# A diffusion-transformer layer on one core: a written order for the gate/up chunks, the down-projection split by stream, and the latent values moved

## The chip, the core and the metric

The kernel runs on one core of a Trainium2 chip. The metric is the device time of one execution in microseconds (us), as the median of several runs. The core has five engines that work side by side, each through its own instruction queue in order: TensorE (matrix products, "PE" in the profile, its weight loads "PEld"), VectorE ("DVE"), ScalarE ("ACT"), GpSimd ("POOL") and SyncE ("SP"), which here issues all DMA transfers. Sixteen DMA engines move data between the chip's main memory (DRAM) and the on-chip memories: SBUF, and PSUM, into which TensorE writes.

## The reference

One layer of a flow-matching backbone over 512 latent tokens and 256 context tokens of width 1024. Every sub-layer is a "sandwich": RMS norm, shift and scale, the sub-layer, RMS norm, gate, residual. Cut to what matters here:

```python
ml = adaln(c, w_mod, b_mod)         # silu(c) @ w_mod + b_mod: nine vectors of 1024, latent tokens
mc = adaln(c_ctx, w_mod, b_mod)     # the same for context tokens (vectors 0 to 4 are used)
h  = x   + 0.5 * gate * rms_norm(swiglu(modulate(rms_norm(x,   g), shift, scale)), g2)   # FFN 1
hc = ctx + 0.5 * gate * rms_norm(swiglu(modulate(rms_norm(ctx, g), shift, scale)), g2)   # same weights
k_c, v_c = split_kv(modulate(rms_norm(hc, g), ...) @ w_in[:, K and V columns])
u = modulate(rms_norm(h, g), ...) @ w_in          # q, k, v and the gated convolution's inputs
h = h + gate * rms_norm(token_mixer(u, k_c, v_c)) # 8 heads, two softmax maps each, over 768 keys
h = h + 0.5 * gate * rms_norm(swiglu(...))        # FFN 2, latent tokens only
```

The FFN's hidden width is 2816, 22 chunks of 128. All is float32. A product is made of three passes with a high and a low part of each operand: high x high, high x low, low x high.

## The kernel before

**Splitting.** `unit` (L74) loads 512 KB of weights into a tile `wraw` (four buffers). `split` (L80) makes `whi` on ScalarE (`hi`, L62) and `wlo = wraw - whi` on VectorE (`lo`, L67), or on GpSimd for every n-th unit when `pool_share` is n.

**Who sets the order.** The program is written as one sequence, and generators (`take`, `drain`) weave side work into it. A planner then puts each engine's instructions in order at build time: by priority, which falls with the place in the text, among those that its own estimate of durations holds ready. So the order of an engine's queue can differ from the text, and is fixed when the program runs. `tc.issue_after` adds edges where the author wants them.

**Gate/up of FFN 1** (L541 to L626). Latent and context tokens are one operand of 768 columns, used as halves of 384. Chunks 0 and 1 are plain (`plain_tail`, L532). From chunk 2 on, a Strassen-like scheme needs seven products of 12 matmuls (`product`, L569) instead of eight. It takes four weight operands, made from the gate raw `rg` and the up raw `ru`: `rg` itself, a difference written over half of `ru`, the pair `s12`, and `s4`. `weights1` and `weights2` (L543 to L559) form them with four GpSimd operations (L548 to L551) and split them. The products accumulate in three PSUM tiles A (`pa`), K (`pb`) and G (`pc`); copies `n1`, `n7`, `n6` (L583, L597, L599) keep states that a later product accumulates over. `tail` (L619) runs the seventh product of a chunk in the next iteration, and `spill` (L464) writes the hidden chunk as `hh` and `hl` to `hf_dram`.

**Conditioning sums** (`mod_steps`, L474). The modulation vectors 2 to 8 are matrix-vector products that VectorE makes: `macc = mraw * scalar + macc` (L490), 512 columns at a time, two columns blocks q for each vector m, for the latent (v=0) and, for m up to 4, the context stream (v=1). TensorE adds over the partitions with a matrix of ones; VectorE then multiplies by an identity matrix (L512) and reduces (L516), which turns the summed row into columns. Vectors 2 to 4 are made in the gate/up loop, 5 to 8 in the first part of the down-projection.

**Down-projection of FFN 1** (`down`, L658). Two passes over the 22 chunks. Part 1 makes all eight output blocks for the context (256 columns) and latent blocks 0, 1, 2 (512 columns); part 2 makes latent blocks 3 to 7, with 640 of 1024 weight columns, and beside it the context's chain runs.

**The chain** (`sandwich`, L1149): norm, gate and residual for eight blocks, a second norm, then modulation into high and low parts. Most of its steps are VectorE and ScalarE work with two short visits to TensorE per norm (`rstd_steps`, L107).

**Context keys and values** (L709 to L747). `kv_ctx_k` for 8 heads, then `kv_ctx_v` for 4 pairs of heads, with the latent chain beside them (`pool_share` 2).

**Attention** (L750 to L947). `gen_v` (L779) makes the latent values of a pair of heads, `gen_qk` its keys and queries, `gen_conv` the convolution branch; a running budget (`slot`, `due`) spreads this work over 32 score blocks.

## Time and profile before

| | us |
|---|---|
| median of 3 runs (1700.87 to 1707.27) | 1704.58 |
| the profiled execution | 1702.55 |
| its span in the profile | 1700.5 |
| gate/up loop, 92 to 422 | 330 |
| down-projection, part 1, 422 to 561 | 139 |
| down-projection, part 2, 561 to 641 | 80 |
| context keys and values, 641 to 710 | 69 |
| attention, 710 to 1079 | 369 |
| the rest of the layer, 1079 to 1700.5 | 621.5 |

TensorE is busy 1597.5 us (94%), VectorE 1070.5 (63%), ScalarE 711.1 (42%), GpSimd 324.4 (19%). The stages were cut at the first and last matmuls of their output tiles. A row of a timeline is: start, duration, engine, line, operation, output from inputs, count, and in brackets how long the engine stood idle before and what released it. A row of the instruction groups ends with the total busy time, the mean in ns, and the idle time before them. A row of the waits gives who waited for whom, the total in us, how often, and the longest. A row of DMA issues gives the size of one and the median us from issue to landing. Because matmuls are pipelined, a TensorE that shows as busy can still be slower than its best; the spacing of starts tells.

### The profile page before, as it was taken

The page shows a single profiled execution, that of the slowest core. Times are in us where ns is not written, and L with a number is a line of the kernel's source. Part 1 is how long each engine was busy: PE and PEld are TensorE (multiplying, and loading weights), DVE is VectorE, ACT ScalarE, POOL GpSimd, SP SyncE. Part 2 cuts the span into 40 slices and gives each one's busy share as a digit, 9 for nine tenths or more (in the row PEclk, how much of TensorE's full clock was granted, in tenths as well). Part 3 has the DMA queues.
Part 4 walks back from the last instruction along what each step waited for, and adds up shares of the span by engine and source line. Part 5 has one row for each costly group of instructions (what it writes and reads, how often), then busy time and mean ns, then how long its engine had stood idle before and what let it go on. Part 6 is the DMA issues. An engine that isn't in the chain of part 4 may idle for free. (4 is left out here: it accounts for less than half of the span.)

```text
span 1700.5 us, 23561 instructions
## 1 busy us (share of the span) xinstructions
PE 1597.5 (94%) x8962; PEld 1423.9 (84%) x8962; DVE 1070.5 (63%) x1492; ACT 711.1 (42%) x1125; POOL 324.4 (19%) x241
## 2 busy tenths in 40 slices
PE   5989999998988997999999999999999999999996
PEld 4889989898867786978888988878889998888886
DVE  5698889874566637677777776473347844333345
ACT  4543444344111434545555555452237732222234
POOL 3555555562000105310000000000002100000003
PEclk9989999999999997999999999999999999999998
DMA  9144444435898885874544453643246743232321
GB/s 366 45 154 156 149 167 151 160 120 170 313 320 320 288 279 180 259 206 118 155 130 143 118 146 103 217 150 103 95 135 200 246 151 112 84 114 91 92 79 50
DMA packets 117583, 281.98 MB, mean 166 GB/s; under 512 B 12768, under 2 KB 43616, under 8 KB 117472
## 3 DMA queue, kind: packets, MB, share of 16 engines
q1 hardware_dynamic: 117472, 280.50, 50.8%
q8 instruction: 70, 1.15, 0.3%
q14 instruction: 41, 0.34, 0.1%
HBM read 233.79 MB, written 34.08 MB: 158 GB/s over the span
## 5 line engine op out<-in xcount | busy, mean ns | idle before, releaser
L62 ACT CAST whi<-wraw 128x1024 fp32r<-128x1024 f32 (+2 forms) x266 | 266.5, 1004 | 513.7 <-PE pa L90 94.9
L67 DVE TENSOR_TENSOR wlo<-wraw,whi 128x1024 fp32r<-128x1024 f32 (+2 forms) x258 | 327.1, 1269 | 189.0 <-ACT whi L62 177.4
L90 PE MATMUL f<-xs,whi 128*128 128x512 f32 x640 | 199.9, 393 | 0.0
L90 PE MATMUL pa<-xs,whi 128*128 128x512 f32 (+1 forms) x704 | 195.8, 361 | 0.8 <-ACT ob L900 0.5
L90 PEld LDWEIGHTS pa<-xs,whi 128*128 128x128 f32 x704 | 126.1, 189 | 21.2 <-ACT ob L900 0.7
L490 DVE SCALAR_TENSOR_TENSOR macc<-mraw,sc,macc 128x512 f32<-128x512 f32 x140 | 131.1, 963 | 11.3 <-DMA mraw<-wmodr 10.0
L90 PEld LDWEIGHTS f<-xs,whi 128*128 128x128 f32 x640 | 118.1, 188 | 23.1
L90 PE MATMUL pa<-xs,wlo 128*128 128x512 f32 (+1 forms) x352 | 127.0, 361 | 1.5 <-DVE wlo L67 1.5
L90 PE MATMUL f<-xs,wlo 128*128 128x512 f32 x320 | 124.9, 390 | 0.0
L143 POOL TENSOR_TENSOR sqacc<-sqacc,sqt 128x256 f32<-128x256 f32 (+1 forms) x20 | 19.3, 967 | 500.3 <-ACT sqt L141 498.4
L90 PE MATMUL pb<-xs,whi 128*128 128x512 f32 (+1 forms) x448 | 114.4, 344 | 0.0
L676 PE MATMUL c<-hh,whi 128*128 128x256 f32 (+1 forms) x264 | 85.5, 326 | 16.6 <-ACT whi L62 12.6
L676 PE MATMUL c<-hl,whi 128*128 128x256 f32 (+1 forms) x264 | 84.6, 321 | 3.2 <-DMA hl<-hf_dram 3.2
L90 PEld LDWEIGHTS pb<-xs,whi 128*128 128x128 f32 x448 | 78.0, 189 | 10.0
L676 PE MATMUL c<-hh,wlo 128*128 128x256 f32 (+1 forms) x264 | 84.9, 323 | 0.9 <-DVE wlo L67 0.8
L868 ACT ACTIVATE e<-s,mx 128x768 f32<-128x768 f32 x64 | 57.1, 898 | 48.1 <-DVE mx L864 44.8
L90 PE MATMUL pb<-xs,wlo 128*128 128x512 f32 (+1 forms) x224 | 77.1, 344 | 0.0
L766 POOL TENSOR_TENSOR rot<-rot,cossin 128x512 f32<-128x512 f32 x16 | 23.3, 1454 | 280.7 <-DVE rot L765 280.7
L90 PEld LDWEIGHTS pa<-xs,wlo 128*128 128x128 f32 x352 | 66.4, 189 | 11.7 <-DVE wlo L67 1.7
L676 PEld LDWEIGHTS c<-hh,whi 128*128 128x128 f32 x264 | 50.5, 191 | 25.0 <-ACT whi L62 15.1
L90 PEld LDWEIGHTS f<-xs,wlo 128*128 128x128 f32 x320 | 60.1, 188 | 12.9
L574 PE MATMUL pb<-wm,whi 128*128 128x384 f32 x208 | 54.6, 344 | 5.1 <-DVE g L537 5.1
(379 smaller groups left out, 3902.4 us busy)
## 6 DMA issues: line engine op xcount, KB each, us to landing
mraw<-wmodr SPq DMA_DIRECT2D x56, 512.0 KB, 4.3
wraw<-f2gu SPq DMA_DIRECT2D x56, 512.0 KB, 3.6
wraw<-f1gu SPq DMA_DIRECT2D x44, 512.0 KB, 3.5
wraw<-f1d SPq DMA_DIRECT2D x22, 512.0 KB, 5.8
wraw<-f2d SPq DMA_DIRECT2D x24, 384.0 KB, 3.2
hf_dram<-hh SPq DMA_DIRECT2D x22, 384.0 KB, 2.3
hf_dram<-hl SPq DMA_DIRECT2D x22, 384.0 KB, 2.3
hh<-hf_dram SPq DMA_DIRECT2D x22, 384.0 KB, 5.5
```

What stands on the lines that cost most here:

```text
L62: self.nc.scalar.copy(out=out, in_=src)
L67: (eng or self.nc.vector).tensor_tensor(out=out, in0=src, in1=hi.bitcast(F32), op=ALU.subtract)
L90: self.nc.tensor.matmul(out, lhsT=lhsT, rhs=rhs, start=start, stop=stop)
L143: eng.tensor_tensor(out=a, in0=a, in1=s, op=ALU.add)
L490: nc.vector.scalar_tensor_tensor(out=acc[:, v], in0=raw[:, k], scalar=s, in1=acc[:, v], op0=ALU.mult, op1=ALU.add)
L574: self.nc.tensor.matmul(out, lhsT=w, rhs=x, start=start and p + j == 0, stop=p == 3 and j == 2, skip_group_check=True)
L676: nc.tensor.matmul(o, lhsT=w[:, c], rhs=x[hl], start=start and f + j == 0, stop=f == NF - 1 and j == 2, skip_group_check=True)
L766: nc.gpsimd.tensor_tensor(out=rt, in0=rt, in1=cs[:, 1, :], op=ALU.mult)
L868: nc.scalar.activation(e[m], ps[:, m * NKEY:(m + 1) * NKEY], AF.Exp, scale=SCALE, bias=mx[:, 2 + m:3 + m], accum_out=mx[:, 4 + m:5 + m])
```

## The change

**A written order.** `in_order` wraps the gate/up section from the plain tails on. Afterwards it links each instruction of TensorE, VectorE, ScalarE and GpSimd to the one before it on the same engine, so the planner keeps the order of the text on these four. SP's order stays with the planner.

```diff
+    @contextmanager
+    def in_order(self):
+        cur = self.nc.cur_bb
+        n = len(cur.bb.instructions)
+        yield
+        prev = {}
+        for i in cur.bb.instructions[n:]:
+            if i.engine in self.ordered:
+                p = prev.get(i.engine)
+                if p is not None:
+                    self.tc.add_manual_dep(i, p.name, ...)
+                prev[i.engine] = i
```

**Weights of a gate/up chunk** in finer steps. Two of the four GpSimd operations go to VectorE (`w_dve`), and the splits are placed one by one. Chunk 2's weights are begun during the opening products.

```diff
+        def w_pool(f):
+            tt = nc.gpsimd.tensor_tensor
+            tt(out=s12[:, 0], in0=ru[:, :512], in1=ru[:, 512:], op=ALU.add)
+            tt(out=ru[:, :512], in0=rg[:, :512], in1=ru[:, :512], op=ALU.subtract)
+        def w_dve(f):
+            tt = nc.vector.tensor_tensor
+            tt(out=s12[:, 1], in0=s12[:, 0], in1=rg[:, :512], op=ALU.subtract)
+            tt(out=s4, in0=rg[:, 512:], in1=s12[:, 1], op=ALU.subtract)
...
+            if i == 2:
+                w_load(2)
+                w_pool(2)
+                w_dve(2)
+                w_hi(2, 0)
+                w_lo(2, 0)
+                w_hi(2, 2)
+                w_lo(2, 2)
...
+        with self.in_order():
+            plain_tail(0, ps0[0])
+            w_hi(2, 1)
+            w_lo(2, 1)
+            plain_tail(1, ps0[1])
+            cur = begin(2)
...
+                nc.scalar.copy(out=n1, in_=A)
+                if tail:
+                    product(*tail[0])
+                if more:
+                    w_load(f + 1)
+                    w_pool(f + 1)
+                    w_hi(f + 1, 0)
+                    w_lo(f + 1, 0)
+                if tail:
+                    tail[1]()
+                product(K, f, 1, 0, "t3", True)
+                if more:
+                    w_dve(f + 1)
+                if tail:
+                    tail[2]()
+                nc.scalar.copy(out=n7, in_=K)
+                product(A, f, 2, 1, "t2", False)
+                take(mods, 2)
+                if more:
+                    w_hi(f + 1, 2)
+                    w_lo(f + 1, 2)
+                nc.scalar.copy(out=n6, in_=A)
+                product(G, f, 0, 1, "b21", True)
...
+                product(A, f, 2, 0, "t1", False)
...
+                product(K, f, 1, 1, "t4", False)
+                if more:
+                    w_hi(f + 1, 3)
+                    w_lo(f + 1, 3)
+                    cur = begin(f + 1)
...
+                take(mods, 3)
```

Here `tail[0]` is the seventh product of the chunk before, `tail[1]` its silu and GpSimd multiplication, `tail[2]` its spill; `w_hi` and `w_lo` are the two halves of a split.

**Conditioning sums** are cut into an accumulating half (`mod_acc`) and a summing half (`mod_sum`). Vectors 2 and 3 stay in the gate/up loop. Vectors 4 to 8 are accumulated in part 1 of the down-projection and summed in part 2. The summed row is no longer turned by VectorE: ScalarE copies it out, a DMA writes it to DRAM, and another reads it back across the partitions.

```diff
+            row = acc[0:1, :]
+            nc.scalar.copy(out=row, in_=pm[0:1, :])
+            rd = row_dram[m, v]
+            nc.sync.dma_start(out=rd[q:q + 1, :], in_=row)
+            yield
+            if q == 0:
+                return
+            mods = (ml, mcx)[v][:, m * 8:m * 8 + 8]
+            nc.sync.dma_start(out=mods, in_=rd.rearrange("q (i p) -> p (q i)", p=P))
...
+        def mod_late():
+            for m, vs in ((4, (0, 1)), (5, (0,)), (6, (0,)), (7, (0,)), (8, (0,))):
+                for q in range(2):
+                    yield from mod_acc(fp, m, q, vs, 4 if m == 4 else None)
```

**Down-projection by stream.** Part 1 makes the eight latent blocks (eight PSUM banks, full weights, latent columns of `hf_dram`), part 2 the eight context blocks, with the full weights again and the latent chain beside it.

```diff
+        for _ in down(slice(0, 3, 2), [(p, True) for p in pl]):
+            take(mods, 5)
...
+        self.pool_share = 4
+        for f, _ in enumerate(down(slice(1, 2), [(p, d % 2 == 0) for d, p in enumerate(pcs)])):
+            if f > 0:
+                take(chain, 1 if f < 12 else 2)
+            for _ in range(3):
+                next(next(sums, iter(())), None)
```

**Values.** `gen_v` and `kv_ctx_v` give way to `values(q, ts)`, which makes a pair of heads' values for the token blocks `ts` (0 and 1 are context, 2 to 5 latent) and writes them to `v_dram`. It runs between the down-projection and attention, beside the context's chain; attention only loads them (`load_v`). Weights `wv` are read 12 times instead of 16.

```diff
+        self.pool_share = 3
+        for q in range(2):
+            values(q, [2, 3, 4, 5])
+            take(chain, 10)
+        drain(chain)
+        for q in range(2, 4):
+            values(q, [0, 1, 2, 3, 4, 5])
+        for q in range(2):
+            values(q, [0, 1])
         for j in range(NH):
             kv_ctx_k(j)
-            take(chain, 2)
-        for q in range(4):
-            kv_ctx_v(q)
-            take(chain, 4)
-        drain(chain)
...
-        drain(gen_v(0))
+        load_v(0)
```

More of the change, by code (lines that the diff above doesn't have):

```diff
@@ L692, in build @@
[L692 to L706 removed]
+        pl = [self.t(psf, [P, 512], f"b{d}") for d in range(ND)]
@@ new lines, in build @@
+        for d in range(ND):
+            if d % 2:
+                nc.vector.tensor_copy(out=yc[d], in_=pcs[d])
+            else:
+                nc.scalar.copy(out=yc[d], in_=pcs[d])
+            self.sqadd(fp, sqyc, yc[d], d, NCX)
+        for g in sums:
+            next(g, None)
+        drain(chain)
+        xc = [self.t(fp, [P, 2, NCX], f"xc{d}", F32R) for d in range(ND)]
+        xchi, xclo = [t[:, 0, :] for t in xc], [t[:, 1, :] for t in xc]
+        cx = lambda k: (xchi[k], xclo[k])
@@ L930, in build @@
                 prev = (a, at, j, qb)
-                due += slot
+                due += share
                 while due > 0:
```

368 lines of the change are left out of this document (163 added, 205 removed).

## The prediction

> **What bounds the kernel now.** I read the engines' busy time by stage first (columns: stretch, its length, then busy time and instruction count of TensorE, its weight loads, VectorE, ScalarE and GpSimd; granted clock, DMA share, GB/s). The stretches are the gate/up loop of the first FFN, its down-projection's parts 1 and 2, the context's keys and values, and attention; the change leaves the 621 us behind them alone.
>
> ```profile
> 92.00:422.00 330.00, 306.28 (x1692) 301.54 (x1692) 270.16 (x301) 140.85 (x214) 177.02 (x113) 0.97 0.45 154
> 422.00:561.00 139.00, 120.81 (x727) 105.51 (x728) 85.34 (x118) 24.34 (x27) 0.00 (x0) 0.95 0.88 311
> 561.00:641.00 80.00, 79.52 (x364) 65.25 (x362) 40.57 (x81) 30.96 (x55) 9.37 (x10) 1.00 0.88 284
> 641.00:710.00 69.00, 56.66 (x414) 55.27 (x414) 53.53 (x70) 34.20 (x55) 33.82 (x18) 0.85 0.63 203
> 710.00:1079.00 369.00, 366.64 (x2088) 320.09 (x2086) 270.47 (x430) 200.07 (x349) 23.26 (x16) 1.00 0.50 144
> ```
>
> A busy TensorE says little, because matmuls overlap. So I took their pitch from the chain that ended last and from the timeline: 24 in 2.88 us with 256 columns (0.120 each), 24 in 5.44 with 512 (0.227), and one product of 12 with 384 columns from 96.41 to 98.49, 2.08 us.
>
> ```profile
> 1347.16 2.88 PE pa L90 x24
> ...
> 1436.85 5.44 PE pb L90 x24
> ```
> ```profile
> 96.41 0.51 PE L574 MATMUL pa<-xs,whx 128*128 128x384 f32 x2
> ...
> 98.49 0.51 PE L574 MATMUL pc<-xo,whx 128*128 128x384 f32 x2
> ...
> 366.98 0.51 PE L574 MATMUL pc<-xo,whi 128*128 128x384 f32 x2
> ```
> ```profile
> 398.38 0.55 DVE L606 TENSOR_TENSOR g<-n,pc 128x384 f32<-128x384 f32 x1 [1.31 <-PE pc L574]
> ...
> 412.94 0.56 DVE L606 TENSOR_TENSOR g<-n,pc 128x384 f32<-128x384 f32 x1 [1.38 <-PE pc L574]
> ```
>
> Gate/up: a chunk f is seven products, 7 x 2.08 = 14.56 us. The product into pc starts at 98.49 for f=2 and at 366.98 for f=18: 16.78 us a chunk. The last chunks, where the conditioning sums have run out, keep 14.56 exactly (398.38 to 412.94). Over 19 intervals that is (16 x 16.78 + 3 x 14.56) / 19 = 16.43. VectorE tells why:
>
> ```profile
> 369.00:412.90 43.90, 43.90 (x255) 43.90 (x254) 23.72 (x30) 20.29 (x31) 15.59 (x12) 1.00 0.39 130
> 108.00:369.00 261.00, 241.73 (x1332) 237.63 (x1333) 226.09 (x250) 109.83 (x169) 152.94 (x96) 0.97 0.45 154
> ```
>
> With sums it is busy 226.09 of 261 us, 14.5 us a chunk; without, 23.72 of 43.9, 7.9 us. It has no spare time in which to catch up, and accumulating products wait for its evacuations (18.0 us in the first row below). Ahead of the loop TensorE stands idle twice, 2.87 and 5.07 us; the second time VectorE works on the sums for 4.78 us before the multiplication that frees bank pb.
>
> ```profile
> PEld pa L574 <- DVE u L609: 18.0, 8, 4.2
> ```
> ```profile
> 84.50 0.62 PE L574 MATMUL pa<-xe,whx 128*128 128x384 f32 x2 [2.87 <-ACT g L535]
> ...
> 92.58 1.01 PE L574 MATMUL pb<-wm,whi 128*128 128x384 f32 x2 [5.07 <-DVE g L537]
> ```
> ```profile
> 84.68 4.78 DVE L490 SCALAR_TENSOR_TENSOR macc<-mraw,sc,macc 128x512 f32<-128x512 f32 x4
> ```
>
> Down, part 1, is held by transfers: DMA share 0.88, and ScalarE waits 54.0 us for f1d. Part 2 is TensorE's: 22 x 15 x 0.227 = 75 of 80 us. The context's keys and values need 384 x 0.120 = 46.1 us and take 69: the latent chain (norm, residual, modulation) uses the same vector engines, and one stop, of 2.52 us, is shown below, and the stage's clock is 0.85. Attention keeps TensorE busy 366.64 of 369 us.
>
> ```profile
> ACT whi L62 <- DMA wraw<-f1d: 54.0, 11, 10.8
> ```
> ```profile
> 649.47 1.86 PE L90 MATMUL l<-ones,sqacc 128*128 128x1 f32 x8 [2.52 <-DVE sqacc L143]
> ```
>
> **The change, part by part.** The profiled execution took 1702.55 us around its span of 1700.5; the median of the runs is 1704.58, 2.0 more. The sum goes by the former, and 2.0 is added at the end.
>
> Opening. The plain tail of chunk 0 now comes before any sum, and the weights of chunk 2 are made during the opening products. The 2.87 stays (a ScalarE wait). Of the 5.07, about 1.5 stays, because the fixed order puts the split of the weight operand that pb needs between the two tails (a ScalarE copy of 1.05 us, rows below, then VectorE's low half): -3.6 (bounds 0 and -5.1).
>
> Loop. The sums taken here fall from three modulation vectors to two, spread over all 20 chunks: 64 accumulations, 3.2 a chunk. Two subtractions move from GpSimd to VectorE.
>
> ```profile
> L549 POOL TENSOR_TENSOR wraw<-wraw,wraw 128x512 f32<-128x512 f32 x18 | 31.8, 1768 | 1.4
> L548 POOL TENSOR_TENSOR s<-wraw 128x512 f32<-128x512 f32 x18 | 31.2, 1732 | 33.7 <-issue 21.8 <-DMA wraw<-f1gu 5.0 <-DVE wlo L67 3.6
> ...
> L622 POOL TENSOR_TENSOR u<-u,g 128x384 f32<-128x384 f32 x19 | 29.1, 1534 | 38.6 <-ACT g L621 33.8 <-DVE macc L490 4.8
> ```
> ```profile
> L62 ACT CAST whi<-wraw 128x1024 fp32r<-128x1024 f32 x26 | 27.3, 1051 | 24.5 <-PE pc L574 14.2 <-PE pb L574 8.8 <-PE pa L574 1.4
> L62 ACT CAST hh<-u 128x768 fp32r<-128x768 f32 x19 | 15.9, 837 | 27.6 <-POOL u L622 27.6
> ...
> L583 ACT COPY n<-pa 128x384 f32<-128x384 f32 x19 | 9.1, 476 | 15.1 <-PE pa L574 15.0
> ```
> ```profile
> L490 DVE SCALAR_TENSOR_TENSOR macc<-mraw,sc,macc 128x512 f32<-128x512 f32 x78 | 82.9, 1107 | 0.0
> L67 DVE TENSOR_TENSOR wlo<-wraw,whi 128x1024 fp32r<-128x1024 f32 x26 | 40.7, 1566 | 5.5 <-ACT whi L62 5.4
> ...
> L67 DVE TENSOR_TENSOR wlo<-s,whi 128x512 fp32r<-128x512 f32 x12 | 10.1, 838 | 0.0
> ```
>
> VectorE per chunk: 7.9 + 3.2 x 1.107 + 2 x 0.838 for the subtractions + 0.4 x 0.838 for the sums' low halves = 13.5 us, under 14.56, so TensorE sets the pace if the fixed order lets it. The order's tightest place is the copy n6, which the fifth product (t1) waits for, due 4 x 2.08 = 8.32 us after the chunk's start. Ahead of it: two GpSimd operations on the next weights (1.73 + 1.77), the previous chunk's multiplication (1.53), ScalarE's hh (0.84), n7 (0.48), the high half of s12 (1.05), n6 (0.48): 7.88. Spare: 0.44 us. In 8 of 20 chunks a sum puts two more ScalarE operations into this queue. I take 15.0 a chunk: 19 x (16.43 - 15.0) = -27 (bounds: 14.56, -36; 16.78, +7).
>
> Down, part 1, latent columns of all eight blocks: 22 x 24 x 0.227 = 119.7 us of matmul. Bytes from the issues:
>
> ```profile
> mraw<-wmodr SPq DMA_DIRECT2D x56, 512.0 KB, 4.3
> ...
> wraw<-f1gu SPq DMA_DIRECT2D x44, 512.0 KB, 3.5
> wraw<-f1d SPq DMA_DIRECT2D x22, 512.0 KB, 5.8
> ```
> ```profile
> hh<-hf_dram SPq DMA_DIRECT2D x22, 384.0 KB, 5.5
> ```
>
> Before: 22 x (2 x 384 + 512) KB + 32 raws = 45.6 MB. After: 22 x (2 x 256 + 512) KB + 40 raws (modulation 4 to 8) = 44.0 MB. So the stage stays bound by transfers: five steps a chunk give 6.4 chunks at 1.70 MB (TensorE's 5.44 us is longer), 12.8 at 2.36 MB and 2.8 without raws. At a full share, 311 / 0.88 = 353 GB/s, that is 34.8 + 85.6 + 15.2 = 136 us; at 311, 147. I take 137 against 139: -2 (bounds: 44.0 MB / 353, 125 us, -14; +8).
>
> Part 2, context columns: 22 x 2.88 = 63.4 us of matmul and 17.3 MB; the latent residual and its write-back add 4.2 MB. At 284 / 0.88 = 323 GB/s that is 66.6 us, of which some 6 can run during part 1's last 2.8 chunks (15.2 us of matmul, 8.3 of transfer): 60. The latent chain comes in here: three VectorE passes per block at about 0.74 us (the yl row at 740 ns below) plus half the additions, 24 us, with 16.5 low halves of weights at 1.57 and 12 of sums at 0.84, 60 us in all; it hides under TensorE's 63 and the transfers, but barely.
>
> ```profile
> L1171 DVE SCALAR_TENSOR_TENSOR yl<-yl,gp,l x8: 736/740/747, 657.1 to 669.3; 128x512 f32<-128x512 f32 x8
> ```
>
> New here are six reads that turn a summed row into columns, 1,024 elements of 4 bytes each, with a write ahead of each on the same SP queue; four more fall into the loop, whose DMA share of 0.45 hides them. The trace has no such transfer. From below: 1.8 us, the quickest landing. From above: each element costs a mean packet, 0.508 x 16 x 1700.5 / 117472 = 118 ns, so 1024 / 16 x 118 = 7.5 us.
>
> ```profile
> out<-fin SPq DMA_DIRECT2D x16, 128.0 KB, 1.8
> ```
> ```profile
> q1 hardware_dynamic: 117472, 280.50, 50.8%
> ```
>
> I take 2.5, since by bytes they are nearest to the small row: 60 + 6 x 2.5 = 75 against 80: -5 (bounds: 63.4, -17; 105, +25). Four chunks of prefetch, 11.5 us, cover SP's waits for a row. The Trainium skill ("DMA: Bandwidth & Descriptors", Rules for kernel authors) speaks against this edit: a last dimension that isn't contiguous becomes one descriptor per element. By it the price would lie near the upper end; no run here shows it yet.
>
> Keys, values and attention. All of the values' 576 matmuls now stand beside the context's chain: 768 x 0.120 = 92.2 us. The chain is half as wide as the latent one; 23 us of latent values run ahead of its need. I add 6 us for what is left of the stop and its low clock: 98 against 69, +29 (bounds +23, +46). Attention loses 384 of them, 46.1 us:
>
> ```profile
> L90 PE MATMUL f<-whi,xs x256: 278/283/365, 710.6 to 975.4; 128*128 128x256 f32 x128
> ```
>
> TensorE is its bound, so it gives 45 back (bounds -46, -23): -16 net.
>
> Sum: -3.6 - 27 - 2 - 5 - 16 = -54; 1702.55 - 54 = 1649, and 1651 beside the runs' median.
>
> **Rivals.**
> 1. The strided reads cost 7.5 us each and stand in the SP queue ahead of bulk loads: part 2 takes 105, the kernel 1681. For it: DMA share 0.88 there. Against: prefetch, and packets small in bytes. This is where the skill's rule above would lead.
> 2. Slower: the fixed order turns a late weight load into a stop of all engines. If SP issues the load of chunk f+1 only after the raws of the iteration before, two 512 KB loads land some 5 us into the chunk (3.5 + 1.5), GpSimd starts there, and ScalarE's n7 and n6 queue behind it: 14.56 + 5 - 0.44 = 19.1 a chunk, 19 x 4.1 = 78 more, 1729. It decides the sign from 17.8 a chunk (the other gains, 27, over 19). For it: SP waits 88.5 us for weight buffers (row below). Against: GpSimd waited for f1gu for only 5.0 us, and four raw buffers are two chunks.
>
> ```profile
> SPq L267 <- DVE wlo L67: 88.5, 24, 7.6
> ```
> 3. Attention gives back only 23 us, because VectorE (270.47 of 369) and the score chain take over: 1673. Against: with its share of the values gone VectorE has about 254 of 323.
> 4. The order does nothing: the loop stays at 16.4, since the stops by u L609 come from VectorE's place in the queue and not only from its load: 1678. Against: three chunks in the planner's own order already run at 14.56.
> 5. All is hidden: 14.6 a chunk (-8), part 1 in 128 (-9), part 2 in 66 (-9): 1625.
>
> **How the numbers follow.** Forecast 46%, rivals 14, 7, 10, 8 and 15. The likeliest case alone: 1635 to 1668. 1625 to 1692 takes in all but the slower case and sums of two mishaps. This measurement can tell about 0.5%, 8.5 us. Faster 87%, same 6 (two of the costly rivals together), slower 7.
>
> **What would show it.** Right: products into pc 14.6 to 15.3 us apart for f=3 to 20; part 1 at a DMA share near 0.9 in about 137 us; part 2 near 75 with mean landing of the new reads under 4 us; the stage with the values near 98 with clock above 0.9; attention near 324. Wrong: a period above 16, new waits of GpSimd on f1gu, or part 2 above 85.

## The result, and the profile after

The changed kernel takes **1685.81 us** (median of 4 runs, 1684.36 to 1686.69) against 1703.93 for the kernel before (4 runs beside it, 1700.87 to 1707.27): a ratio of **0.989, 95% interval 0.987 to 0.991**. It is faster by 1.1%. The forecast was 1651, a gain of 54 us; the gain is 18. The time lies in the stated range (1625 to 1692), and outside the likeliest case's own (1635 to 1668). The profiled execution took 1684.36 us around a span of 1682.5.

First the stages, read as before (columns as in the prediction's first view: stretch, length, busy time of TensorE, weight loads, VectorE, ScalarE, GpSimd, granted clock, DMA share, GB/s). The rows are the loop from its first product into pc, part 1, part 2, the stage with keys and values, and attention.

```profile
94.70:398.50 303.80, 294.21 (x1662) 288.96 (x1660) 252.62 (x275) 138.04 (x213) 115.76 (x76) 0.99 0.44 148
398.50:535.00 136.50, 126.87 (x534) 99.27 (x535) 88.04 (x118) 23.79 (x27) 0.00 (x0) 0.99 0.90 305
535.00:634.00 99.00, 83.21 (x582) 77.45 (x581) 70.16 (x89) 51.48 (x77) 33.19 (x17) 0.91 0.74 230
634.00:734.00 100.00, 96.50 (x788) 95.82 (x787) 50.47 (x82) 41.74 (x69) 20.73 (x14) 0.98 0.63 203
734.00:1060.00 326.00, 322.33 (x1697) 272.91 (x1697) 252.03 (x405) 185.74 (x324) 21.48 (x16) 1.00 0.56 159
```

| stage, us | before | forecast | after |
|---|---|---|---|
| start to the first product into pc | 98.5 | 94.9 | 94.7 |
| loop, 19 intervals of | 16.43 | 15.0 | 15.31 |
| part 1 | 139 | 137 | 136.5 |
| **part 2** | **80** | **75** | **99** |
| keys and values | 69 | 98 | 100 |
| attention | 369 | 324 | 326 |

Five of six came within about 2% of the forecast, and the sixth, part 2, became 19 us longer where 5 less were forecast. That is 24 of the 36 us that are missing; the loop's 0.31 us a chunk is another 6.

The loop's period is the spacing of VectorE's addition that empties pc (timeline of the changed kernel, first and last of 20):

```profile
97.84 0.55 DVE L671 TENSOR_TENSOR g<-n,pc 128x384 f32<-128x384 f32 x1
...
388.74 0.55 DVE L671 TENSOR_TENSOR g<-n,pc 128x384 f32<-128x384 f32 x1 [2.67 <-PE pc L624]
```

(388.74 - 97.84) / 19 = 15.31. Single intervals run from 14.56 to 17.09. The three longest (16.18, 16.50 and 17.09) hold the products of a conditioning sum; three of 15.9 hold none, but six accumulations each. GpSimd's waits in the loop (who waited for whom, us, times, longest) are on u and g alone, never on f1gu. So the forecast's slower rival, the late weight load, did not come.

```profile
POOL u L685 <- DVE u L684: 190.4, 20, 20.8
POOL u L690 <- ACT g L689: 7.7, 8, 3.8
```

**Inside part 2** a view of 5 us each shows two halves. Chosen rows:

```profile
535.00:540.00 5.00, 0.94 (x5) 0.41 (x3) 5.00 (x5) 3.69 (x7) 4.00 (x3) 0.90 0.91 289
540.00:545.00 5.00, 4.82 (x21) 4.72 (x22) 5.00 (x6) 1.32 (x4) 2.36 (x1) 0.50 0.48 168
...
560.00:565.00 5.00, 2.14 (x10) 2.03 (x10) 5.00 (x5) 2.71 (x4) 3.11 (x3) 0.78 0.57 183
...
570.00:575.00 5.00, 2.00 (x8) 0.83 (x6) 5.00 (x9) 3.42 (x7) 3.03 (x2) 1.00 0.75 161
605.00:610.00 5.00, 5.00 (x44) 5.00 (x44) 2.39 (x3) 1.35 (x2) 1.20 (x1) 1.00 0.77 240
```

```profile
540.18 0.58 PE L731 MATMUL b<-hh,wlo 128*128 128x256 f32 x1 [3.42 <-DVE wlo L67]
```

From 605 us on TensorE makes 44 products in 5 us, the full pace. Before that it stops again and again, and behind a stop the granted clock falls: TensorE stands for 3.42 us until a low half comes at 540.18 (last row, from the timeline), and the window behind it has 21 products, at a clock of 0.50. Over the stage TensorE is idle for 99.0 - 83.2 = 15.8 us, and a mean clock of 0.91 costs about 0.09 x 83 = 7 more (an estimate from that row). The transfers are not the bound: their share, 0.88 before, is 0.74.

Two queues look guilty. SP's issues (timeline) have no load of f1d, the down-projection's weights, between 553.72 and 571.84; in between stand residual loads that wait for a free tile, write-backs and row writes. And the waits of SP's queue in part 2 name the row write behind ScalarE's copy; the longest entry, loads of hidden units (L72) that wait for TensorE to free their tiles, comes of TensorE being late:

```profile
553.72 0.38 SPq L77 DMA_DIRECT2D wraw<-f1d  x1
558.48 0.33 SPq L1228 DMA_DIRECT2D res<-xT  x1
...
564.10 0.34 SPq L1228 DMA_DIRECT2D res<-xT  x1
564.48 0.42 SPq L1245 DMA_DIRECT2D h_dram<-yl  x1
567.98 0.24 SPq L574 DMA_DIRECT2D row_dram<-macc  x1
...
571.84 0.42 SPq L77 DMA_DIRECT2D wraw<-f1d  x1
```
```profile
SPq L72 <- PE b L731: 12.6, 4, 3.6
SPq L574 <- ACT macc L572: 11.7, 3, 6.4
SPq L1228 <- POOL yl L1242: 5.1, 2, 4.3
```

VectorE is busy for 4.3 us or more in nine of the fourteen windows up to 605, and its operations are longer while GpSimd splits a weight tile (timelines of GpSimd, then VectorE; the same sum of squares takes 2.86 us, and 0.68 a little later):

```profile
539.01 3.35 POOL L67 TENSOR_TENSOR wlo<-wraw,whi 128x1024 fp32r<-128x1024 f32 x1
```
```profile
540.05 2.86 DVE L160 TENSOR_TENSOR sqacc<-sqacc,sqt 128x512 f32<-128x512 f32 x1
...
544.64 0.68 DVE L160 TENSOR_TENSOR sqacc<-sqacc,sqt 128x512 f32<-128x512 f32 x1
```

### The profile page after: what moved, and what is told of

Its sections match the earlier page's. It is cut to its first block, busy times and chain, and to the rows that moved or that the text cites. A ratio compares the mean times of both kernels' runs of the same rounds, so it can differ in the third digit from the quotient of the medians.

```text
span 1682.5 us, 23537 instructions
## 1 busy us (share of the span) xinstructions
PE 1598.6 (95%) x8962; PEld 1418.3 (84%) x8962; DVE 1066.9 (63%) x1464; ACT 724.6 (43%) x1137; POOL 268.3 (16%) x205
## 2 busy tenths in 40 slices
DMA packets 135769, 281.16 MB, mean 167 GB/s; under 512 B 23253, under 2 KB 67925, under 8 KB 135657
## 5 line engine op out<-in xcount | busy, mean ns | idle before, releaser
L62 ACT CAST whi<-wraw 128x1024 fp32r<-128x1024 f32 (+1 forms) x262 | 269.4, 1030 | 505.5 <-PE pa L107 95.2
L67 DVE TENSOR_TENSOR wlo<-wraw,whi 128x1024 fp32r<-128x1024 f32 (+1 forms) x250 | 329.4, 1319 | 201.9 <-ACT whi L62 194.5
L731 PE MATMUL b<-hh,whi 128*128 128x512 f32 (+1 forms) x352 | 119.9, 352 | 11.5 <-ACT whi L62 7.9
L731 PE MATMUL b<-hh,wlo 128*128 128x512 f32 (+1 forms) x352 | 112.2, 348 | 11.7 <-DVE wlo L67 6.8
L731 PE MATMUL b<-hl,whi 128*128 128x512 f32 (+1 forms) x352 | 118.4, 343 | 0.6 <-DMA hl<-hf_dram 0.6
L731 PEld LDWEIGHTS b<-hh,whi 128*128 128x128 f32 x352 | 69.7, 199 | 23.9 <-ACT whi L62 13.0
L731 PEld LDWEIGHTS b<-hh,wlo 128*128 128x128 f32 x352 | 65.4, 198 | 22.7 <-DVE wlo L67 10.4
L556 DVE SCALAR_TENSOR_TENSOR macc<-mraw,sc,macc 128x512 f32<-128x512 f32 x84 | 79.8, 1002 | 1.6 <-DMA mraw<-wmodr 1.6
L731 PEld LDWEIGHTS b<-hl,whi 128*128 128x128 f32 x352 | 69.1, 196 | 8.2 <-DMA hl<-hf_dram 1.3
L107 PEld LDWEIGHTS f<-xs,wlo 128*128 128x128 f32 x320 | 60.1, 188 | 12.6
```

The lines of the kernel that those rows point to most:

```text
L62: self.nc.scalar.copy(out=out, in_=src)
L67: (eng or self.nc.vector).tensor_tensor(out=out, in0=src, in1=hi.bitcast(F32), op=ALU.subtract)
L107: self.nc.tensor.matmul(out, lhsT=lhsT, rhs=rhs, start=start, stop=stop)
L556: nc.vector.scalar_tensor_tensor(out=acc, in0=raw[:, k], scalar=s, in1=acc, op0=ALU.mult, op1=ALU.add)
L731: nc.tensor.matmul(o, lhsT=w[:, c], rhs=h[hl], start=start and f + j == 0, stop=f == NF - 1 and j == 2, skip_group_check=True)
```

## The experiments

Theories for part 2: **1**, VectorE's load, with GpSimd's share making it worse; **2**, the sums' matmuls in TensorE's in-order queue over one PSUM bank; **3**, waits in SP's queue (3a residual loads, 3b row writes); **4**, the strided reads' own time (the prediction's rival 1). Lengths come from one profile each, part 2 from its first product to the first product of the values: 99.6 us in the changed kernel by this measure, behind 135.7 of part 1. Where only one run was made, the kernel's time is that run's; the kernel before took 1700 to 1708 beside them. Differences under some 2 us in one profile are not told apart. Part 1 took between 135.7 and 140.3 us in runs that left it as it was, so the two parts together (235.3 in the changed kernel) are given where they say something else than part 2 alone.

**One cause at a time.** Four runs, each with one thing taken away.

```diff
-        self.pool_share = 4
+        self.pool_share = 0
```

> In part 2 of the down-projection GpSimd no longer takes every fourth low half of the weights; VectorE takes them all (about 6 more at 1.22 us, 7.3 us). In the changed kernel these GpSimd operations take 2.7 us each and VectorE operations beside them stretch (2.86, 2.50 and 2.38 us where the same form takes 0.7). Theory 1 (VectorE is the bound of the first twelve chunks and GpSimd's share costs it more than it saves): part 2 falls from 98 us by 6 to 10. Theory 2 (the sums' matmuls, in TensorE's queue over one bank) and theory 3 (loads held back in SP's queue behind row writes and residual loads): part 2 stays within 3 us, or grows by up to 7 if VectorE is the bound and the stretching is not real.

Measured: part 2 97.0, kernel 1681.71. The share costs a little more than it saves; alone it is not the loss.

```diff
-            nc.sync.dma_start(out=rd[q:q + 1, :], in_=row)
+            if m < 4:
+                nc.sync.dma_start(out=rd[q:q + 1, :], in_=row)
...
-            nc.vector.tensor_tensor(out=mods, in0=mods, in1=...)
+            nc.vector.tensor_tensor(out=mods, in0=mods if m < 4 else acc[:, 0:8], in1=...)
```

> The sums of modulation vectors 4 to 8 are not turned into columns through DRAM: 12 row writes and 6 strided reads leave SP's queue in part 2, and the addition of the bias takes its values straight from the accumulator (this leaves out the turning of the sums, so the modulations of the second half are not the reference's). All else stays. Theory 3 (row writes wait in SP's queue for ScalarE's copies and hold f1d and hidden-unit loads behind them): part 2 falls by 10 us or more, and the gap of 18 us without a load of f1d is gone. Theory 4 (the strided reads' own transfer, rival 1 of the prediction): part 2 falls by 6 x 7.5 = 45 us at most, and the DMA share falls with it. Theories 1 and 2: within 4 us.

Measured: part 2 90.4, kernel 1677.41. The rows' trip costs 9 of the 24 us by part 2's length; over both parts it is 4.8 (230.5), because part 1 took 140.1 here. The gap in the loads of f1d shrinks to 12.6 us and does not go. Whether the trip costs by waits or by transfers, the row writes below tell in part.

```diff
-   mod_sum(fp, psf, "b4", 1, m, q, 0)
+   mod_sum(fp, psf, f"b{(4, 6, 7)[(2 * m + q) % 3]}", 1, m, q, 0)
```

> The sums' matmuls take turns on three free PSUM banks where they share one. Theory 2 (a sum's matmul in TensorE's in-order queue waits until ScalarE has copied the sum before out of the one bank): part 2 falls by 5 us or more. Theories 1 and 3: within 3 us.

Measured: part 2 100.4, kernel 1683.06. Theory 2's bank is not it.

```diff
+            if m > 4:
+                if q == 0:
+                    return
+                mods = ml[:, m * 8:m * 8 + 8]
+                nc.vector.tensor_tensor(out=mods, in0=acc[:, 0:8], in1=..., op=ALU.add)
...
+                return
```

> The eight sums of modulation vectors 5 to 8 are left out of part 2 altogether: their splits, 16 matmuls, copies, row writes and reads (their accumulation in part 1 stays; the modulations 5 to 8 are not the reference's). It takes away about 8 x 0.82 us of VectorE, 8 x 1.2 us of ScalarE, 16 places in TensorE's queue and 12 transfers in SP's. Whatever the way in which they cost (theories 1 to 3), part 2 falls to 80 to 85 us, that is by 13 to 18, with the four sums of vector 4 left. If it stays above 92, the sums are not the cause and it is the latent chain beside the context's columns.

Measured: part 2 **96.7**, kernel 1685.12. Eight of twelve sums gone, and next to nothing gained, over both parts nothing (236.8): so the sums are not the loss by themselves. SP's timeline of this run has the same gap: no load of f1d for 17 us, and residual loads in it.

```profile
560.85 0.38 SPq L77 DMA_DIRECT2D wraw<-f1d  x1
...
566.64 4.69 SPq L1241 DMA_DIRECT2D res<-xT  x3
...
577.49 0.42 SPq L77 DMA_DIRECT2D wraw<-f1d  x1
```

**SP's queue, edit by edit.** Residual loads get eight tiles (four borrowed from `kch` and `vch`); row writes go to ScalarE's queue; then both and no GpSimd share; then the sums 5 to 8 placed behind the chain.

```diff
-   xhi, xlo, NT, h_dram, lambda d: ("res", 4))
+   xhi, xlo, NT, h_dram, lambda d: res8(d))
...
-            nc.sync.dma_start(out=rd[q:q + 1, :], in_=row)
+            (nc.scalar if m > 3 else nc.sync).dma_start(out=rd[q:q + 1, :], in_=row)
...
+            for _ in range(4 if f > 11 else 0):
+                next(next(sums2, iter(())), None)
```

> The latent residual's eight loads get a tile each (four of them in tiles that the next stage uses later for keys and values), so that none waits in SP's queue for a tile that the chain must first empty. The experiment without the eight sums showed that gap in SP's queue most plainly: no load of f1d between 560.85 and 577.49 us, with three residual loads at 566.64 to 571.33. Theory 3a (these waits hold f1d and hidden-unit loads back): part 2 falls from 98 us by 7 to 13, and no load of f1d is more than 10 us behind the one before while the chain runs. Theory 1 (VectorE's load alone, about 65 of the first 71 us): within 3 us.

> The 12 row writes of part 2 are issued from ScalarE's queue, right behind the copy that they wait for, in place of SP's; the strided reads stay on SP. Theory 3b (it is the row write, waiting in SP's queue for ScalarE's copy, by which the rows cost their 9 us): part 2 falls by 5 to 9 us, as it did without the rows' trip. If it is the strided reads or the bytes: within 3 us. Theory 1: within 3 us or slower, since ScalarE takes on 12 issues.

> Eight residual tiles, rows written from ScalarE's queue, and no low halves on GpSimd in part 2, together. If the waits in SP's queue are what part 2 lost (theory 3), it takes 77 to 84 us, close to the 75 forecast, and the kernel 1662 to 1670 us. If VectorE's load sets it (theory 1), 92 or more.

> The same, and the eight sums of modulation vectors 5 to 8 come in the last ten chunks of part 2, behind the latent chain, where VectorE is busy 11 of 28 us in the changed kernel. Theory 3 alone: as the run with the three edits, within 3 us. With theory 1 for the rest (chain, weights and sums meet in VectorE in the first half): 3 to 8 us less than that run, part 2 at 72 to 78.

Measured, part 2 and kernel: residual tiles 98.4 and 1681.82; row writes 95.8 and 1677.58; all three **87.1** and 1672.32; sums behind the chain 89.9 and 1675.11. Alone the three edits take 1.2, 3.8 and 2.6 us off, 7.6 in sum; together 12.5 (over both parts 0.8, 3.3 and 1.0, and 9.4 together).

That looks like more than the sum, but one stop stands in the way of the comparison. At the crossing TensorE waits for part 2's first low half: 3.42 us in the changed kernel and 3.2 to 3.3 in the runs above without GpSimd's share, but 6.3 in the runs with the tiles alone and the row writes alone, and in those with three banks and without the eight sums. There GpSimd's split comes first, VectorE's sum of squares beside it takes 2.82 us, and the low half stands behind it (timelines of GpSimd, VectorE and TensorE in the run with the tiles):

```profile
537.07 2.46 POOL L67 TENSOR_TENSOR wlo<-wraw,whi 128x1024 fp32r<-128x1024 f32 x1 [0.30 <-ACT whi L62]
```
```profile
537.24 2.82 DVE L160 TENSOR_TENSOR sqacc<-sqacc,sqt 128x512 f32<-128x512 f32 x1
539.99 1.21 DVE L67 TENSOR_TENSOR wlo<-wraw,whi 128x1024 fp32r<-128x1024 f32 x1
```
```profile
541.25 0.58 PE L731 MATMUL b<-hh,wlo 128*128 128x256 f32 x1 [6.26 <-DVE wlo L67]
```

With a stop as short as the changed kernel's, 2.8 us less, the tiles would be worth 4.0 and the row writes 6.6, and the three would add up to 13.2 (estimates from these lengths), about the 12.5 measured together. So this stop is enough to make theory 3a look dead when tried by itself. The tiles did what they were for: while the chain runs, no load of f1d is more than 8 us behind the one before. The gap that is left, 17.7 us, lies at the crossing, where the row write waits 8.7 us for ScalarE's copy. How much one wait hid of another cannot be told from these lengths. Yet 87.1 is above the 77 to 84 that theory 3 gave. Placing the sums later brought nothing.

**More of the same, and the loop's order.** The write-backs too leave SP's queue; besides, part 2's first weights come ahead of part 1's evacuations, or the eight sums are left out. And the changed kernel with its fixed order switched off.

```diff
-            if i.engine in self.ordered:
+            if False and i.engine in self.ordered:
...
-                nc.sync.dma_start(out=h_out[d], in_=y[d])
+                nc.scalar.dma_start(out=h_out[d], in_=y[d])
...
+        ahead = [self.unit(io["f1d"][f]) for f in range(2)]
```

> The changed kernel with the fixed order of the gate/up loop taken out: TensorE's order stays, VectorE, ScalarE and GpSimd go back to the planner's. The sums are spread as in the changed kernel (two vectors over 20 chunks). If the order is what brought the loop from 16.43 to 15.35 us a chunk, the loop goes back to 16.2 or more: down-projection starts 16 to 25 us later than at 398.5, kernel 1700 to 1710. If the lighter sums did it and the order does nothing (rival 4 of the prediction in another form): within 4 us of 398.5.

> Eight residual tiles, row writes from ScalarE's queue, no GpSimd share, and now the eight write-backs of the latent residual too are issued from ScalarE's queue, behind the square that waits for the same value. In the run with the first three edits they held SP's queue for 8 us (6.3 us at 549.5, where the next loads came at 556). Theory 3: part 2 falls from 87 by another 3 to 7 us, to 80 to 84. Theory 1 (what is left of the loss is VectorE, full from 560 to 575 us): within 2 us of 87.

> As the run before, and part 2's first two weight tiles are loaded and split ahead of the eight evacuations of part 1. In the changed kernel TensorE does 0.94 of 5 us at 535 to 540 and waits 3.4 us for the first low half, which stands behind evacuations and sums of squares in VectorE's queue. If the crossing from part 1 to part 2 is a stop of its own: 3 to 5 us less than the run before over parts 1 and 2 together. If the work only moves: within 1.5 us.

> As the run without chain waits on SP, and the eight sums of vectors 5 to 8 left out as before (their modulations are not the reference's). Alone, leaving them out did nothing, since SP's queue was held anyway. If VectorE's and TensorE's load by the sums (theories 1 and 2) is the rest of the loss, it shows now: part 2 falls by 5 to 10 us against the run with the sums, to 72 to 77. If it stays within 2 us, the rest is the chain itself.

Measured, **order**: kernel 1686.49, the down-projection starts at 399.9; the loop keeps its pace without it (timeline, first and last addition from pc):

```profile
101.66 0.54 DVE L671 TENSOR_TENSOR g<-n,pc 128x384 f32<-128x384 f32 x1
...
390.93 0.55 DVE L671 TENSOR_TENSOR g<-n,pc 128x384 f32<-128x384 f32 x1 [1.86 <-PE pc L624]
```

(390.93 - 101.66) / 19 = 15.22, against 15.31 with the order. Single intervals vary more (12.96 to 19.06), their mean does not. TensorE's order is the same in both traces; the fixed order of the other three does nothing for the time. So something else in the change brought the loop from 16.43. VectorE's lighter load is the likeliest (the views of stages give 12.7 us a chunk where it was 13.5), but no run takes it apart from the finer splits and from the two operations that left GpSimd. Part 2, which this run leaves as it is, takes 102.4 us, with the longer stop of 6.3 at the crossing.

Part 2: write-backs off SP 88.1 (no gain on 87.1), weights ahead 88.3, without the eight sums **83.2** (kernels 1676.44, 1676.37, 1668.62). The weights ahead only moved work: both parts together took 226.7 us against 225.3. So SP's queue has no more to give. The sums, worth 2.9 us in the first setting, are worth 4.9 here; the run behind the 2.9 has the longer stop at the crossing, which is all of the difference and more. The rest is something else.

**The sums in another form.** Four products of a 128-column block of the accumulator with one column of ones give the sum as columns: no split, no row, no DRAM.

```diff
-            al = self.t(pool, [P, 2, 512], "mraw", F32R, bufs=2)
...
+            for i in range(4):
+                self.mm(pm[:, i:i + 1], acc[:, i * P:(i + 1) * P], self.ones[:, 0:1], True, True)
+            nc.vector.tensor_tensor(out=mods[:, c0:c0 + 4], in0=pm[:, :4],
+                                    in1=vec[:, V_BM + c0:V_BM + c0 + 4], op=ALU.add)
...
-            for m, vs in ((4, (0, 1)), (5, (0,)), (6, (0,)), (7, (0,)), (8, (0,))):
+            for m, vs in ((4, (0, 1)), (7, (0,)), (8, (0,))):
```

> The changed kernel, but each conditioning sum is made by four products of a 128-column block of the accumulator with one column of ones, so that the sum comes out of PSUM as columns: no split into high and low halves, no copy of a row, no row write, no strided read; one addition per half vector. All 20 sums, in the loop and in part 2. It leaves in place the residual loads on four tiles, the write-backs on SP and GpSimd's share. If the 12 sums' whole trip is worth what the two runs showed apart (9 us without the rows' trip; 5 us more without eight sums where SP is free), part 2 falls from 99.6 by 9 to 14 us, and the loop by up to 8 (eight sums with 16 matmuls and 16 ScalarE operations, which the prediction priced at 15.0 - 14.56 a chunk). If only SP's queue counts, the loop stays within 2 us.

> The same with eight residual tiles, write-backs from ScalarE's queue and no GpSimd share. If waits in SP's queue and the sums are together what part 2 lost, it takes 76 to 82 us (the run without sums 5 to 8 took 83.2, with four sums in the old way left), the kernel 1660 to 1668. If it stays at 83 or more, the crossing from part 1 to part 2 and the chain's own operations in VectorE's queue are the rest.

> The same, and modulation vectors 5 and 6 (16 of part 1's 40 raw loads, 8.4 of 44.0 MB) are accumulated and summed beside the keys and values in place of part 1. If transfers bound part 1, as the prediction had it, the 35.6 MB take 108 us at 330 GB/s, less than TensorE's 120: part 1 falls from 137 to 121 to 126 us. The stage with the values, with VectorE busy 50 of 100 us and 203 GB/s there, stays within 3 us. Kernel 1645 to 1655. If part 1 is not bound by transfers, it stays above 132.

Measured: columns alone, kernel 1673.27, part 2 98.7 (with 7.3 us of stop at the crossing) and not 9 to 14 us less, but the **loop** 8.3 us shorter (14.91 a chunk). With SP free and no GpSimd share 1674.49 (1672.79 to 1676.35), part 2 92.6 where 76 to 82 was expected, ratio 0.984 (0.982 to 0.986). With vectors 5 and 6 moved **1647.39** (1644.41 to 1653.75, 4 runs, against 1701.44, 7 runs), ratio **0.968 (0.966 to 0.971)**, faster than both kernels. Its stages: part 1, part 2 (first product 514.97, first of the values 589.91: **74.9 us**), keys and values.

```profile
390.90:514.90 124.00, 121.66 (x528) 100.25 (x529) 70.72 (x90) 26.38 (x29) 0.76 (x1) 0.99 0.92 321
514.90:590.00 75.10, 74.50 (x627) 74.25 (x626) 60.26 (x86) 38.54 (x52) 17.73 (x12) 1.00 0.80 266
590.00:695.00 105.00, 98.92 (x817) 98.50 (x816) 66.57 (x111) 39.16 (x66) 20.92 (x14) 0.98 0.73 238
```

Part 1 falls by 11.6 us, from 135.7 to 124.1, as expected. The edit takes 16.6 us of VectorE's work out of it too, so the length alone would not name the cause; but ScalarE's wait for f1d in it, in the changed kernel as below, is gone, so transfers did bound it. The stage with keys and values took 105 us and not 100 give or take 3.

```profile
ACT whi L62 <- DMA wraw<-f1d: 69.9, 11, 11.5
```

Part 2, with the chain inside, runs with no stop over 0.6 us at a clock of 1.00. The kernel with one-column products below has the same part 2 and takes 75.4 us for it. The kernel with free SP and the old place of the vectors shows what is new in the column form: right behind a row of such products (two records each), with TensorE never idle for over 0.3 us, the clock falls.

```profile
540.84 1.03 PE L107 MATMUL b<-ones,macc 128*128 128x1 f32 x8
542.13 1.05 PE L107 MATMUL b<-ones,macc 128*128 128x1 f32 x8 [0.26 <-DVE mcx L570]
543.44 1.19 PE L107 MATMUL b<-ones,macc 128*128 128x1 f32 x8 [0.26 <-DVE ml L570]
```
```profile
542.00:544.00 2.00, 1.62 (x13) 1.53 (x14) 0.41 (x3) 1.18 (x2) 0.00 (x0) 1.00 1.01 347
...
546.00:548.00 2.00, 1.75 (x9) 1.66 (x9) 0.16 (x1) 1.04 (x1) 0.00 (x0) 0.50 0.01 4
```

**The two causes left: the chain itself, and the clock.**

```diff
-            if f > 0:
-                take(chain, 1 if f < 12 else 2)
...
+                n = {8: 40, 14: 10}.get(f, 0)
+                for _ in range(n):
+                    self.mm(pm[:, 0:1], self.ones, self.ones[:, 0:1], True, True)
```

> The changed kernel, but the latent chain (norm, residual, modulation) gives no step during part 2 and runs whole behind it, ahead of the values; the twelve sums stay in part 2 in their old form. If it is the meeting of chain and context products, with the residual loads and write-backs in SP's queue, that part 2 lost by, its products now take 70 to 76 us from the first to the last (63.4 and the sums' own matmuls, 12 x 2 x 0.23 = 5.5), and the chain costs 30 us or more behind them, so that the kernel is slower than the changed one by 5 to 15 us. If the sums alone make the loss, part 2 stays above 88.

> The same and the eight sums of vectors 5 to 8 left out (their modulations are not the reference's): with neither, part 2's products take 66 to 70 us. Together with the run without these sums alone (96.7) and the run before it gives the four corners: if the two losses simply add, leaving out the sums is worth 3 us here too; if each hides behind the other, it is worth more here than the 3 there.

> In the kernel with columns, free SP and two vectors later (1647.4 us), chunk 8 of the gate/up loop gets 40 more products of one column, and chunk 14 gets 10, all on constants. At 0.12 us each they take 4.8 and 1.2 us of TensorE by themselves. In the run with the sums as columns the granted clock fell to 0.50 from 544 to 554 us, right behind 38 such products in 5 us, with TensorE never idle for over 0.3 us. If such products lower the clock as a stop does, the clock falls below 0.7 for some 10 us behind the 40 and chunk 8 takes 8 to 11 us more in all; behind the 10 it stays at 1.00. If the fall there had another cause, the clock stays at 1.00 in both places and chunk 8 takes 4.8 us more.

Measured, **chain behind part 2**: the products of part 2 take **76.2 us** with all twelve sums in their old form (first product 538.58, last 614.79), and the chain 32.5 behind them; kernel 1699.15. Without the eight sums 76.0, where 66 to 70 was expected; kernel 1696.14. This run has the longer stop at the crossing (6.25 us, against 3.19 with the sums), so the sums cost some 3 us without the chain too (an estimate), about as much as with it. In the first of these two runs the gap in the loads of f1d is gone with the chain: the longest is 8.0 us. The same stretch in four more kernels, by the view of stages: three edits on SP and GpSimd; SP free and no eight sums; column sums alone; no chain.

```profile
536.50:623.60 87.10, 78.11 (x585) 73.22 (x586) 69.88 (x95) 52.56 (x78) 17.93 (x11) 0.98 0.82 256
```
```profile
536.50:619.80 83.30, 74.33 (x569) 72.02 (x570) 63.29 (x83) 45.13 (x61) 19.31 (x11) 0.94 0.87 287
```
```profile
526.80:625.50 98.70, 86.92 (x651) 85.85 (x650) 56.35 (x86) 41.24 (x58) 30.39 (x17) 0.88 0.72 240
```
```profile
538.60:614.90 76.30, 72.15 (x552) 70.20 (x553) 41.75 (x50) 39.28 (x58) 18.14 (x8) 0.96 0.80 241
```

Each length is TensorE's busy time plus its idle time, and the busy time holds what the clock lost. Idle it is for 9.0, 9.0, 11.8 and 4.2 us, at clocks of 0.98, 0.94, 0.88 and 0.96 (15.8 at 0.91 in the changed kernel). Busy time multiplied by the clock is 69 to 77 us in all of them, and 74.5 in the kernel with two vectors later, which has neither long stops nor a slow clock.

**One-column products**: kernel 1666.61. The loop's interval with the 40 in it is 30.02 us where it was 14.63, the one with the 10 17.02 where it was 14.76. The records (two for each such product) and the clock around the 40 and the 10:

```profile
192.96 15.13 PE L107 MATMUL pd<-ones 128*128 128x1 f32 x80
207.95 0.99 PE L617 MATMUL pa<-xo,whi 128*128 128x384 f32 x2
```
```profile
194.00:196.00 2.00, 2.00 (x16) 2.00 (x16) 2.00 (x2) 0.58 (x1) 1.92 (x2) 0.77 0.59 182
196.00:198.00 2.00, 2.00 (x11) 2.00 (x11) 2.00 (x2) 0.00 (x0) 0.58 (x1) 0.50 0.23 88
...
210.00:212.00 2.00, 2.00 (x8) 2.00 (x8) 0.00 (x0) 0.00 (x0) 0.00 (x0) 0.50 0.00 0
212.00:214.00 2.00, 2.00 (x13) 2.00 (x12) 0.00 (x0) 0.71 (x2) 1.01 (x1) 0.96 0.01 4
```
```profile
300.00 2.37 PE L107 MATMUL pd<-ones 128*128 128x1 f32 x20
```
```profile
302.00:304.00 2.00, 2.00 (x14) 2.00 (x14) 1.97 (x3) 0.00 (x0) 0.00 (x0) 1.00 0.00 0
```

The 10 take 2.37 us, 0.24 each and not the 0.12 expected, and the clock stays at 1.00 behind them. (The expectation counted records as products: its 38 in 5 us are 19.) The 40 would take 9.5 at that pace; they take 15.1, and the 384-column products behind them run at half pace until 212. The clock fell some 2 us after the first of them and came back 4 us after the last. Of the 15.4 us more, where 8 to 11 were expected, 9.5 are the products' own and about 6 the clock's; the next interval is another 1.6 us longer (15.45 where it was 13.86).

## Why the prediction was right or wrong

**Opening**: right. -3.6 forecast, 98.49 to 94.73 is -3.8.

**Loop**: the size came near; the trust in the fixed order was misplaced, and the bound (VectorE's load, relieved by taking out one vector of three and spreading the rest) fits the runs but is not shown by one. Rival 4 said that the order does nothing and that the loop therefore stays at 16.4; the first half is true, the second false. The term that was too small is the sum: I gave 0.44 us a chunk for everything beyond 14.56 and measured 0.75. In the column form, without splits, row copies and 16 wide matmuls, the loop gives back 8.3 us and keeps 14.91, so the eight sums in row form carry more than the whole 0.31 by which the step missed.

**Part 1**: right in size (137 forecast, 136.5) and in cause: with 8.4 MB less the wait for f1d ended and the stage became shorter. It took 124.1 then, within the 121 to 126 that I expected of that run.

**Part 2** is the step that failed, at two sentences. "It hides under TensorE's 63 and the transfers, but barely" compared totals: 60 us of VectorE work beside 63 of matmuls. The work is a chain, and with it in place the stage takes 99.6 us, without it 76.2. That this is close to the 75 forecast is luck: the 75 was 60 us of transfers and 15 of strided reads, and the 76.2 are TensorE's, busy for 72.15 of them at a DMA share of 0.80. The total said nothing about order: the chain, the weights' low halves and the sums share in-order queues, and a late low half stops TensorE. "Four chunks of prefetch, 11.5 us, cover SP's waits for a row" failed likewise: there was no load of f1d for 18 us (553.72 to 571.84), because residual loads that wait for the chain stand in the same queue as the bulk loads. I had counted their bytes and not their waits. Of the 23.4 us that the chain costs, 12.5 went with SP's waits and GpSimd's share, and 4 to 5 more with eight sums. What is left, some 7 us, I ascribe to VectorE's and TensorE's queues and the clock behind each stop; that part is argued, not shown. None of it is a price that the chain must cost: with two vectors later part 2 takes 74.9 us with the chain inside. The floor of 63.4 was also short: the sums' own 24 matmuls (12 x 2 x 0.227 = 5.5 us) were not in it, and no kernel here went below 74.9.

**Strided reads** (rival 1): refuted. One in part 2 of the changed kernel, where the rival put them, issue and use:

```profile
608.76 0.37 SPq L579 DMA_DIRECT2D ml<-row_dram  x1
```
```profile
612.99 0.17 DVE L581 TENSOR_TENSOR ml<-ml,vec 128x8 f32<-128x8 f32 x1 [1.79 <-DMA ml<-row_dram]
```

That is 4.2 us from issue to use, with VectorE standing idle for the last 1.79. The six of part 2 land 2.5 to 4.2 us behind their issue, 3.4 in the mean, and this one is the slowest. Three of the four in the loop take 2.2. So the price in part 2 is above the 2.5 taken and far from 7.5. The rule of the Trainium skill ("DMA: Bandwidth & Descriptors", Rules for kernel authors), one descriptor per element, is no contradiction. The trace agrees with it (packets under 512 B rise from 12,768 to 23,253, and ten reads of 1,024 elements are 10,240), but at 1,024 elements the price stays small. Leaving the rows' whole trip out gained 9 us in part 2 all the same (4.8 over both parts). The waits around it are part of this: the write alone, taken off SP, gave 3.8. How the rest divides was not tested.

**Keys, values, attention**: right, 100 and 326 against 98 and 324. TensorE is the bound of both, and attention gave back 43 of the 46 us; rival 3 (23 back) is refuted.

**The sum**: -54 forecast, -18 measured. Part 2 is 24 us of the difference, the loop 6 to 7, values and attention together 4. The kernel with one vector pair moved shows that part 2 can hold the chain in 75 us. Against the kernel at 92.6 its trace has 7.2 us less idle time (half of it the stop at the crossing, 4.23 us there), 16 one-column products fewer (3.8 us at 0.24), and some 7 us less lost to the clock (84.8 us busy at 0.91 there; an estimate). Which of the edit's effects does it (four sums fewer in part 2, no accumulations left over at its start, no row of one-column products) was not separated, nor why its stage with the values takes 105 us.

## What to carry to other kernels

Work put beside a bound engine is hidden only if its waits are, too: for each queue that it enters, ask what stands behind a waiting instruction, the DMA queue first, and give loads that wait for consumers a queue or tiles of their own. Totals of busy time can show that something does not fit; they cannot show that it fits. When one edit out of several suspects gains nothing, compare its trace with the other stop by stop before dropping the suspect, and try the suspects together: here 1.2, 3.8 and 2.6 us alone were 12.5 together, and a stop that two of the single runs had 2.8 us longer is enough to explain it.

## What the hardware showed that I had not expected

**The clock falls on thin work, not only on idle time.** Forty one-column products, back to back, brought the granted clock to 0.50 within some 2 us; ten did not. The Trainium skill ("TensorE: Matmul & The Clock Gate", Part 1: The HAM clock gate) has the clock halved after an idle window of about 3.4 us and restored after as long a busy one. The trace agrees that a stop halves the clock, but not with the times as counted from the stop: in the stop of 3.42 us ahead of 540.18 the clock was at 0.50 from 538.95, 2.2 us into it, to 545.78, 5.6 us after it; with the one-column products it fell 2.1 us behind the first and came back 4 us behind the last. And the runs add that products of one column lower the clock as a stop does. So a stop costs more than its own length.

**GpSimd's split of a weight tile holds up VectorE**: 2.86 us for an operation of 0.68. The Trainium skill ("SBUF — State Buffer", SBUF: two separate sides) says that the two engines share a port pair which one of them locks for a whole instruction; the trace agrees (GpSimd's split ends at 542.36, and VectorE's operation, begun at 540.05, at 542.91). Handing every fourth tile to GpSimd gained nothing: without it part 2 was 2.6 us shorter. It costs twice: TensorE waits for GpSimd's own low halves (4.8 us in part 2, three times), and VectorE's lengthened operation can stand ahead of a low half that TensorE waits for, as at the crossing above.
